# A hybrid encoder layer on one core: the mixer's blocks in another order, and an output operator kept in float32

## The chip, the cores and the metric

The kernel runs on one core of one Trainium2 chip, as one program launch. The metric is device time in microseconds (us): 1196.42 us is the median of 3 runs of the kernel before (1193.84 to 1198.22 us). Five engines each work through a queue of their own: TensorE (PE; its weight loads are listed apart as PEld), VectorE (DVE), ScalarE (ACT), GpSimd (POOL) and SyncE (SP). They wait for each other by semaphores, and an instruction that waits holds everything behind it on its engine. Transfers (DMAs) are issued from the queues of SP, ACT or POOL and run on 16 DMA engines.

## What is computed

One encoder layer over 512 tokens of width 1024: a SwiGLU feed-forward half step, a mixer with two parallel branches, a second feed-forward half step, and a per-layer embedding. The change lies in the mixer:

```
u = RMSNorm(h);  [q|k|v|x_ssm|g_attn|g_ssm] = u @ W_in        # 512,128,128,512,1024,1024 columns
y_attn = BlockGQA(AxialRoPE(RMSNorm(q)), AxialRoPE(RMSNorm(k)), v) @ W_attn_branch   # 8 q heads, 2 kv heads, of 64
z      = gelu(S5_fwd(x_ssm) + S5_bwd(x_ssm) + D*x_ssm)        # 32 groups of 16 channels, 64 complex states
y_ssm  = (z * sigmoid(z @ W_glu + b_glu)) @ W_ssm_branch
h      = h + (sigmoid(g_attn)*y_attn + sigmoid(g_ssm)*y_ssm) @ W_out
```

Everything is float32. The large products run in three passes (the helper `mm3`, L567): each operand is split into a rounded high part and the rest, and high x high, high x low and low x high are added up in PSUM.

## The kernel before

The layer runs in stages: FFN1 (the first 400 us or so of the trace; the parameters of the SSM are prepared beside it, and its operators written to DRAM), the in-projection with the mixer (to about 740 us), FFN2, and the embedding. All activations are kept transposed, features on the 128 partitions and 512 tokens along the free dimension.

**Tiles.** A weight chunk (`wchunk`, L556) is a 128 x 1024 float32 tile: SP issues its load, ACT casts the high part (L554), DVE subtracts for the low part (L555). There are 4 raw buffers and 4 high/low ones. A *gate* (L829) is one 128-column tile of g_attn or g_ssm: 24 matmuls of 128 x 512 (`pi`, L569 to L571), a DVE multiply into `ta` or `ts` (L833) and an ACT tanh (L834). There are 16 gates: 8 `ta`, 8 `ts`.

**The SSM.** The 32 groups are worked in 16 blocks of two (`ssm_prefetch` L436, `ssm_block` L453). A block loads its operators through SP: `wv` (L441), tables `tbl` (L444, L445), `wol` (L447) and `ml` (L449). PE makes `pv` from the input `U` and `wv` (24 products of 64 columns, six bf16 products for one float32 product, `mm6`). DVE rotates it (L471 to L473), runs two prefix scans (L481, L482) and rotates back (L485 to L487) into `E`. `split3` (L31) cuts E into three bf16 parts: ACT cast, DVE subtract `Er` (L34), ACT cast, DVE subtract (L36). PE then adds `U` x `ml` and `E` x `wol` in `py` (12 and 24 products), and ACT applies gelu into `Z`.

**The order of the mixer.** x_ssm, k and v and then q are projected; q and k are normalised and rotated. In program order there follow 8 gates, the transposes of q and k, the 16 blocks with one gate behind each of blocks 0, 2, 4 and 6, and the scores of head 0 behind block 14. `Z` is stored to DRAM (`zs_d`, 8 SP DMAs, L983), to come back with channels on the partitions (`zT`, L1032). Then come 8 heads; beside the values of head i and the scores of head i+1 runs `fill(i)`: four gates, the two halves of the GLU product and two of the four chunks of the SSM branch. Behind the heads stand the other two chunks of the SSM branch, the four of the attention branch (each merged in `attn_done`), W_out, FFN2 and the embedding.

**A head.** `scores` (L942): for each of 4 query tiles two matmuls `sc`, a row maximum `nb` on DVE (L957), a small DVE multiply by the query's norm `rq` (L958), and an exponential on ACT with bias `nb` and scale `rq` (L960). `values` (L988): 4 x 4 transposes `ppt`, their split `ph` (ACT) and `pl` (DVE), and 8 matmuls `po`. After every second head the reciprocals of the row sums go to DRAM (`r_d`, L966) and come back spread over 64 partitions (`R`, L1016), to scale the heads' output, which is then split into `oT`.

**What sets the order.** Each engine's queue is laid out by the scheduler of the language's Tile layer: it goes through the program with a timeline of its own and takes what is ready by it, earlier program order first; `tc.high_priority()` puts the blocks ahead. So code order and queue order differ, and the rows under the change show the queues. A tile with `bufs=1` can be loaded again only when the last reader of the old content is done.

Of the kernel before, what the change touches and what calls it, by code (L numbers as in the profile page):

```python
# [45 lines left out]
def ssm_params(tc, nc, pk_, px, dp, k):  # L46
# [6 lines left out]
    d["wo"] = dp.tile([NB, P, 3 * GB * 2 * P], BF16, name="d_wo")  # L53
# [264 lines left out]
    bds = [pw.tile([P, 2, GB, 2, CH], F32, name=f"bd{i}") for i in range(2)]  # L318
# [18 lines left out]
    for b in range(NB):  # L337
# [3 lines left out]
        wt = pw.tile([P, GB, 2, L, CH], F32, tag="wt", name=f"wo{b}")  # L341
# [20 lines left out]
        bd3 = pw.tile([P, 3, 2, GB, 2 * CH], BF16, tag="bd3", bufs=2, name=f"bd3{b}")  # L362
# [50 lines left out]
    for b in range(NB):  # L413
# [5 lines left out]
        wt = pw.tile([P, GB, 2, P], F32, tag="wt", name=f"wv{b}")  # L419
# [16 lines left out]
def ssm_prefetch(nc, sp, k, j):  # L436
# [81 lines left out]
def kernel(  # L518
# [331 lines left out]
    with tc.tile_pool(name="qp", bufs=1, reuse_waits="tile") as qp:  # L850
# [93 lines left out]
    def scores(hd):  # L944
# [25 lines left out]
    Z = sp.tile([P, G, NC_], F32, tag="U", name="Z")  # L970
    for j in range(NM):
        with tc.high_priority():
            py = ssm_block(nc, sp, ps, pre, U3, j)
        if j < NM - 1:
            pre = ssm_prefetch(nc, sp, kd, j + 1)
        S.activation(Z[:, j * GM:(j + 1) * GM].rearrange("p g c -> p (g c)"), py[:, :GM * NC_], AF.Gelu_apprx_tanh)
        if j % 2 == 0 and j // 2 < NG2:
            run(gate(NG1 + j // 2))
# [239 lines left out]
```

## Time and profile before

| | before |
|---|---|
| median of 3 runs | 1196.42 us (1193.84 to 1198.22) |
| the profiled execution | 1192.81 us |
| its span, first to last instruction | 1191.0 us |
| mean granted TensorE clock | 0.985 of full |
| PE busy | 1144.2 us (96%) |
| DVE busy | 772.2 us (65%) |
| ACT busy | 505.7 us (42%) |

The profile is one execution; its span is 1.8 us shorter than its own time, which is 3.6 us below the median. An engine is busy while it runs an instruction; waits, register and DMA-issuing instructions don't count. A row of waits names the engine and line that waited, and what came last. Line numbers are those of the kernel before, and "L43", "L36" and "L555" are lines in helpers, which is why the tile names matter more.

### The profile page before, as it was taken

How to read it: one execution, taken by the hardware profiler on the slowest of the kernel's cores; microseconds unless marked ns; L12 is line 12 of the kernel's file. 1: busy time of each engine (PE TensorE's matmuls, PEld its weight loads, DVE VectorE, ACT ScalarE, POOL GpSimd, SP SyncE). 2: the span in 40 equal slices, each digit the busy share in tenths (PEclk: the TensorE clock that was granted, in tenths of full speed). 3: DMA queues.
4: the chain of work that ended last, by engine and by line, in shares of the span. 5: the costliest groups of instructions: out<-in, count | busy, mean ns of one | idle time of the engine just before them, and what ended most of it. 6: DMA issues, size and time to landing. Idle time of an engine off the chain costs nothing.

```text
span 1191.0 us, 16469 instructions
## 1 busy us (share of the span) xinstructions
PE 1144.2 (96%) x6150; PEld 944.3 (79%) x6150; DVE 772.2 (65%) x1574; ACT 505.7 (42%) x917; POOL 44.1 (4%) x71
## 2 busy tenths in 40 slices
PE   8999979999999998998896999999999999999998
PEld 7888768888788887877675788888888888888886
DVE  4987789877589848998665857554443344444542
ACT  6484455445345436443565634333222223223331
POOL 1314200000000000000000000000000000000100
PEclk9999989999999999998997999999999999999999
DMA  8739856545968996886532125333223433223422
GB/s 193 165 100 302 255 192 204 160 141 113 268 228 264 302 177 190 232 267 201 144 69 57 45 78 174 93 94 101 85 66 97 141 89 106 79 72 98 154 59 53
DMA packets 258496, 175.97 MB, mean 148 GB/s; under 512 B 38928, under 2 KB 239824, under 8 KB 258416
## 3 DMA queue, kind: packets, MB, share of 16 engines
q1 hardware_dynamic: 252880, 157.41, 46.9%
q0 software_dynamic: 3920, 11.15, 3.5%
q10 hardware_dynamic: 1616, 6.36, 1.5%
q8 instruction: 48, 0.79, 0.3%
q14 instruction: 32, 0.26, 0.1%
HBM read 148.89 MB, written 37.58 MB: 157 GB/s over the span
## 4 chain that ended last, share of the span: by engine, by line
PE 76%; DMA 9%; DVE 5%; ACT 4%; SPq 3%; issue 2%; ACTq 0%; DVEq 0%
PE pg L569 7%; PE pg L570 7%; PE pg L571 7%; PE pd L569 7%; PE pd L571 7%; PE pd L570 7%; PE pu L571 5%; PE pu L569 5%; PE pu L570 5%; DMA ml<-d_m 3%; PE pi L569 2%; DMA d_tb<-tst 2%; PE pi L570 2%; PE pi L571 2%; SPq L411 1%
## 5 line engine op out<-in xcount | busy, mean ns | idle before, releaser
L723 DVE TENSOR_TENSOR t<-pu,rb 128x512 f32<-128x512 f32 x44 | 30.3, 689 | 84.6 <-PE pu L571 84.4
L721 DVE TENSOR_TENSOR t<-pg,rb 128x512 f32<-128x512 f32 x44 | 30.2, 687 | 51.6 <-PE pg L571 49.3
L554 ACT CAST ah<-t 128x512 fp32r<-128x512 f32 x44 | 27.4, 622 | 39.4 <-DVE t L724 38.5
L741 DVE SCALAR_TENSOR_TENSOR h<-pd,h 128x512 f32<-128x512 f32 x32 | 22.0, 687 | 30.4 <-PE pd L571 30.4
L722 ACT ACTIVATE t<-t 128x512 f32<-128x512 f32 x44 | 27.9, 633 | 24.3 <-DVE t L721 23.5
L555 DVE TENSOR_TENSOR pl<-ppt,ph 128x512 fp32r<-128x512 f32 x32 | 21.9, 684 | 17.6 <-ACT ph L554 17.6
L555 DVE TENSOR_TENSOR al<-t,ah 128x512 fp32r<-128x512 f32 x44 | 30.1, 685 | 4.2 <-ACT ah L554 4.0
L724 DVE TENSOR_TENSOR t<-t,t 128x512 f32<-128x512 f32 x44 | 30.3, 688 | 2.4
L960 ACT ACTIVATE p<-sc,nb,rq 128x512 f32<-128x512 f32 x32 | 24.8, 781 | 6.9 <-DVE nb L958 6.8
L554 ACT CAST ph<-ppt 128x512 fp32r<-128x512 f32 x32 | 18.6, 588 | 15.8 <-PE ppt L1000 15.4
L1123 POOL DMA_DIRECT2D pin<-in_p_dram x8 | 4.2, 530 | 556.1 <-PE pd L570 551.0
L1005 PE MATMUL po<-ph,vhl 128*128 128x512 f32 x32 | 14.0, 439 | 10.9 <-ACT ph L554 10.8
L579 ACT ACTIVATE xh<-h,gains 128x512 fp32r<-128x512 f32 x24 | 17.4, 723 | 16.7 <-DVE h L741 16.3
L957 DVE TENSOR_REDUCE nb<-sc 128x1 f32<-128x512 f32 x32 | 21.4, 682 | 1.0 <-PE sc L956 0.7
L43 PE MATMUL py<-U,ml 128*128 128x64 bf16 x192 | 10.8, 197 | 10.2 <-DMA ml<-d_m 10.2
L1000 PE MATMUL ppt<-ident,p 128*128 128x128 f32 x128 | 20.2, 272 | 0.2 <-ACT p L960 0.2
L1000 PEld LDWEIGHTS ppt<-ident,p 128*128 128x128 f32 x128 | 16.2, 140 | 4.4 <-ACT p L960 0.3
L580 DVE SCALAR_TENSOR_TENSOR xl<-h,gains,xh 128x512 fp32r<-128x512 f32 x24 | 17.9, 746 | 0.4
L43 PE MATMUL py<-E,wol 128*128 128x64 bf16 x384 | 17.6, 196 | 0.4 <-DVE E L36 0.4
L43 PEld LDWEIGHTS <-wv 128*128 128x128 bf16 x384 | 12.9, 100 | 6.1 <-issue 5.4
L43 PE MATMUL pv<-U,wv 128*128 128x64 bf16 x384 | 14.6, 196 | 3.2 <-DVE U L36 3.2
L43 PEld LDWEIGHTS <-ml 128*128 128x128 bf16 x192 | 7.8, 100 | 11.3 <-DMA ml<-d_m 11.1
(1970 smaller groups left out, 3892.2 us busy)
## 6 DMA issues: line engine op xcount, KB each, us to landing
w<-in_ffn_w_gate_dram SPq DMA_DIRECT2D x44, 512.0 KB
w<-in_ffn_w_up_dram SPq DMA_DIRECT2D x44, 512.0 KB
w<-in_w_in_dram SPq DMA_DIRECT2D x26, 512.0 KB
w<-in_ffn_w_down_dram SPq DMA_DIRECT2D x32, 384.0 KB
w<-in_ffn_w_down_dram SPq DMA_DIRECT2D x32, 320.0 KB
d_wo<-wo SPq DMA_DIRECT2D x8, 768.0 KB
d_wv<-wv SPq DMA_DIRECT2D x8, 768.0 KB
wv<-d_wv SPq DMA_DIRECT2D x16, 384.0 KB
```

The lines of the kernel that those rows point to most:

```text
L43: nc.tensor.matmul(o, a[i], b[j], start=start and n == 0, stop=stop and n == 5)
L554: S.copy(hi, src)
L555: V.tensor_sub(lo, src, hi.bitcast(F32))
L569: T.matmul(o, ah, bh, start=start, stop=False)
L570: T.matmul(o, ah, bl, start=False, stop=False)
L571: T.matmul(o, al, bh, start=False, stop=stop)
L721: V.tensor_mul(t1, gu[0], rb)
L722: S.activation(t1, t1, AF.Silu)
L723: V.tensor_mul(t2, gu[1], rb)
L724: V.tensor_mul(t1, t1, t2)
L960: S.activation(p_, sc, AF.Exp, bias=nb[:, t:t + 1], scale=rq[:, t, hd:hd + 1], accum_out=sm[:, t:t + 1])
L1000: T.transpose(pt[:, t * P:(t + 1) * P], pr[t][:, kt * P:(kt + 1) * P], ident)
```

## The change

Five things are changed.

1. **Output operator.** `d_wo` is kept in float32 (256 KB a block to load where it was 384 KB) and E is not split: a block has 4 float32 products with `wol` where it had 24 bf16 ones. `wv` has two buffers (before one). In the preparation `wt` has two buffers, and `bd` and `bd3` one instead of two.
2. **Query norm.** q is multiplied by `rq` (4 DVE multiplies of 128 x 512) before the transposes. The multiply of each row maximum by `rq` and the scale of the exponential are gone.
3. **Order.** 4 gates, then 12 SSM blocks with a gate behind every third of them (gates 4 to 7); block 0 is held back until the last q matmul is issued; then the q and k transposes, the last 4 blocks and the scores of head 0. Beside head i runs gate 8 + i. Behind the heads: `z_load`, the attention branch, the GLU, the SSM branch, which now merges (`ssm_done`).
4. **Store of Z.** In four groups of blocks, each of 8 DMAs of 16 x 8 x 64, 32 in all.
5. **Queues.** `zs_d`, `r_d`, `R`, `zT` and the reload of `h` are issued by POOL, no longer by SP.

```diff
-    d["wo"] = dp.tile([NB, P, 3 * GB * 2 * P], BF16, name="d_wo")
+    d["wo"] = dp.tile([NB, P, GB * 2 * P], F32, name="d_wo")
...
-    wv = sp.tile([P, 3, GM, 2 * P], BF16, tag="wv", name=f"wv{j}")
+    wv = sp.tile([P, 3, GM, 2 * P], BF16, tag="wv", bufs=2, name=f"wv{j}")
...
-    E3 = [sp.tile([P, 2, N], BF16, tag=f"E{i}", bufs=2, name=f"E3{j}_{i}") for i in range(3)]
-    split3(nc, sp, E, E3, "vv", f"Er{j}", 3)
...
-            mm6(nc, o, [wo[:, i, g, ri * P:(ri + 1) * P] for i in range(3)],
-                [e[:, ri, g * NC_:(g + 1) * NC_] for e in E3], False, ri == 1)
+            nc.tensor.matmul(o, wo[:, g, ri * P:(ri + 1) * P], E[:, ri, g * NC_:(g + 1) * NC_],
+                             start=False, stop=ri == 1)
...
-        for m in range(NG1):
+        for t in range(TT):
+            V.tensor_mul(qs[t], qs[t], rq[:, t].unsqueeze(2).broadcast_to([P, NH, HD]))
+        for m in range(KT // 2):
             run(gate(m))
+        def ssm(j):
+            nonlocal pre
+            with tc.high_priority(), (tc.issue_after(last_q.ins) if j == 0 else ExitStack()):
+                py = ssm_block(nc, sp, ps, pre, U3, j)
...
+            if j % 4 == 3:
+                gs = slice((j - 3) * GM, (j + 1) * GM)
+                for l in range(L):
+                    nc.gpsimd.dma_start(zv[l][:, gs], Z[l * CH:(l + 1) * CH, gs])
+        for j in range(NM - JL):
+            ssm(j)
+            if j % 3 == 0:
+                run(gate(KT // 2 + j // 3))
...
-            V.tensor_mul(nb[:, t:t + 1], nb[:, t:t + 1], rq[:, t, hd:hd + 1])
-            S.activation(p_, sc, AF.Exp, bias=nb[:, t:t + 1], scale=rq[:, t, hd:hd + 1], accum_out=sm[:, t:t + 1])
+            S.activation(p_, sc, AF.Exp, bias=nb[:, t:t + 1], accum_out=sm[:, t:t + 1])
...
-            nc.sync.dma_start(r_d[hd // 2].rearrange("h (t p) -> p h t", p=P), s2)
+            nc.gpsimd.dma_start(r_d[hd // 2].rearrange("h (t p) -> p h t", p=P), s2)
...
-                nc.sync.dma_start(R[i * HD:(i + 1) * HD], r_d[hd // 2][i].partition_broadcast(HD))
+                nc.gpsimd.dma_start(R[i * HD:(i + 1) * HD], r_d[hd // 2][i].partition_broadcast(HD))
...
-            nc.sync.dma_start(zT, zs_d[m * P:(m + 1) * P])
+            nc.gpsimd.dma_start(zT, zs_d[m * P:(m + 1) * P])
...
     for hd in range(NH):
-        run(values(hd), fill(hd), *([scores(hd + 1)] if hd < NH - 1 else []))
-    for i in range(NH, 2 * KT - NG1 - NG2 + 6):
-        run(fill(i))
+        run(values(hd), gate(KT + hd), *([scores(hd + 1)] if hd < NH - 1 else []))
+    z_load()
     for mc in range(4):
         run(half(w["w_attn_branch"][0], mc, ohl, attn_done))
+    for mc in range(2):
+        run(half(w["ssm_glu_w"][0], mc, [z[1:] for z in zs[1:]], glu_done))
+    for mc in range(4):
+        run(half(w["w_ssm_branch"][0], mc, yhl, ssm_done))
```

**PE where the first block begins.** Before, block 0's first products stand in the middle of the 96 matmuls `pq` of the q projection (the last 48 of them follow):

```order
L571 MATMUL pq_4518<-w_330h,xl_373 128x512
L569 MATMUL pq_4518<-w_330h,xh_374 128x512
L570 MATMUL pq_4518<-w_330l,xh_374 128x512
L571 MATMUL pq_4518<-w_330h,xl_375 128x512
L43 LDWEIGHTS wv_4150
L43 MATMUL pv_5068<-U_4161,wv_4150 128x64
L43 LDWEIGHTS wv_4150
L43 MATMUL pv_5068<-U_4160,wv_4150 128x64
...
L43 LDWEIGHTS ml_5160
L43 MATMUL py_5244<-U_4159,ml_5160 128x64
L569 MATMUL pq_4515<-w_331h,xh_376 128x512
L570 MATMUL pq_4515<-w_331l,xh_376 128x512
```

Now they stand behind the last `pq`, block 0 and block 1 (the second `wv`) in turn:

```order
L569 MATMUL pq_4518<-w_332h,xl_381 128x512
L567 MATMUL pq_4518<-w_332h,xh_382 128x512
L568 MATMUL pq_4518<-w_332l,xh_382 128x512
L569 MATMUL pq_4518<-w_332h,xl_383 128x512
L43 LDWEIGHTS wv_4150
L43 MATMUL pv_4863<-U_4161,wv_4150 128x64
L43 LDWEIGHTS wv_4920
L43 MATMUL pv_4963<-U_4161,wv_4920 128x64
```

The products that read `U` moved from the middle of the q projection to its end, and the first two blocks are interleaved. (The next rows of both are more of the same 24 products, then those with `ml`.)

**The queue that carries r_d, R and zT.** Before, on SP, from the load of the first two zT tiles on (weights `w` stand in between):

```order
L1032 DMA zT_7220<-zs_d 128x512
L1032 DMA zT_7226<-zs_d 128x512
L966 DMA r_d_5064<-s_428_6890 128x8x1
L1032 DMA zT_7232<-zs_d 128x512
L1032 DMA zT_7238<-zs_d 128x512
L1016 DMA R_7209<-r_d_5064 64x512 x2
L564 DMA w_7824<-in_w_attn_branch_dram 128x4x256
L564 DMA w_7874<-in_w_attn_branch_dram 128x4x256
L966 DMA r_d_5065<-s_483_7122 128x8x1
L1016 DMA R_7494<-r_d_5065 64x512 x2
```

Now, on POOL, from the second `r_d` on:

```order
L989 DMA r_d_5898<-s_420_6331 128x8x1
L1029 DMA R_6638<-r_d_5898 64x512 x2
L989 DMA r_d_5899<-s_475_6555 128x8x1
L1029 DMA R_6862<-r_d_5899 64x512 x2
L989 DMA r_d_5900<-s_530_6779 128x8x1
L1042 DMA zT_7068<-zs_d 128x512
L1042 DMA zT_7074<-zs_d 128x512
L1042 DMA zT_7080<-zs_d 128x512
L1042 DMA zT_7086<-zs_d 128x512
L1029 DMA R_7060<-r_d_5900 64x512 x2
```

Before, two of the four zT stand behind the second `r_d`; now all four stand directly behind the fourth, and ahead of the last `R`. No weights stand in this queue.

**ACT where the z tiles are cast.** Before, beside heads 2 and 3 (`p` is the exponential, `ph` the cast of transposed probabilities, `ob` the copy of a head's upper half):

```order
L960 ACTIVATE p_7088,s_428_6890<-sc_7083,nb_7008,rq 128x512
L554 CAST oT_6981<-of_6860 128x512
L554 CAST z_7222<-zT_7220 128x512
L554 CAST w_617h<-w_7626 128x1024
L554 CAST z_7228<-zT_7226 128x512
L834 ACTIVATE ts_5059<-ts_5059 128x512
L554 CAST z_7234<-zT_7232 128x512
L554 CAST ph_7047<-ppt_7042 128x512
L554 CAST z_7240<-zT_7238 128x512
L554 CAST ph_7071<-ppt_7066 128x512
L960 ACTIVATE p_7128,s_483_7122<-sc_7123,nb_7121,rq 128x512
L960 ACTIVATE p_7152,s_483_7122<-sc_7147,nb_7121,rq 128x512
```

Now, beside the last two heads:

```order
L552 CAST ph_6876<-ppt_6871 128x512
L552 CAST w_618h<-w_7194 128x1024
L552 CAST z_7070<-zT_7068 128x512
L1024 COPY ob_6859<-po_6755 64x512
L552 CAST ph_6907<-ppt_6902 128x512
L833 ACTIVATE ts_5893<-ts_5893 128x512
L552 CAST z_7076<-zT_7074 128x512
L552 CAST z_7082<-zT_7080 128x512
L552 CAST z_7088<-zT_7086 128x512
L552 CAST oT_6866<-of_6749 128x512
L552 CAST ph_6930<-ppt_6925 128x512
L552 CAST ph_6953<-ppt_6948 128x512
```

The four casts `z` moved from there to the last two heads, and casts `ph` that the last products `po` read stand behind them: one behind the first z, the others behind all four.

## Rows read from the trace of the kernel before

**Rows 1.** The page: busy us, share and instructions; PE clock in 40 slices.
```profile
PE 1144.2 (96%) x6150; PEld 944.3 (79%) x6150; DVE 772.2 (65%) x1574; ACT 505.7 (42%) x917; POOL 44.1 (4%) x71
PEclk9999989999999999998997999999999999999999
```
**Rows 2.** Windows: us, busy of each engine (instructions), clock, DMA share, GB/s.
```profile
456.00:581.00 125.00, 114.34 (x1286) 96.01 (x1284) 112.94 (x268) 56.11 (x154) 0.76 (x1) 0.96 0.75 222
490.00:510.00 20.00, 18.14 (x230) 14.82 (x228) 19.53 (x62) 7.83 (x15) 0.00 (x0) 1.00 0.96 281
...
530.00:550.00 20.00, 15.04 (x170) 13.30 (x167) 17.64 (x39) 8.11 (x18) 0.00 (x0) 0.83 0.66 201
...
624.00:641.00 17.00, 5.53 (x14) 3.73 (x13) 5.57 (x13) 3.75 (x8) 0.00 (x0) 0.60 0.37 69
641.00:705.00 64.00, 63.13 (x311) 50.99 (x311) 46.76 (x80) 37.73 (x71) 0.00 (x0) 1.00 0.23 58
820.00:960.00 140.00, 140.00 (x619) 115.99 (x618) 57.34 (x70) 37.38 (x46) 0.00 (x0) 1.00 0.33 97
```
**Rows 3.** What PE waited for, 408 to 700 us: total, times, longest.
```profile
PE po L1005 <- ACT ph L554: 10.8, 2, 10.5
PE py L43 <- DMA ml<-d_m: 10.2, 7, 3.5
PE pv L43 <- DVE U L36: 3.2, 1, 3.2
```
**Rows 4.** What the SP queue waited for, whole span.
```profile
SPq L1016 <- DMA r_d<-s: 38.0, 4, 10.3
...
SPq L444 <- DVE te L485: 32.5, 12, 5.3
```
**Rows 5.** DVE by line, 456 to 581 us: busy, mean ns | idle before.
```profile
L36 DVE TENSOR_TENSOR E<-Er,E 128x256 bf16<-128x256 f32 x16 | 6.7, 421 | 1.2 <-ACT E L35 1.0
L34 DVE TENSOR_TENSOR Er<-vv,E 128x256 f32<-128x256 f32 x16 | 6.7, 419 | 3.1 <-ACT E L33 3.1
L833 DVE TENSOR_TENSOR ta<-pi,rb 128x512 f32<-128x512 f32 x8 | 5.5, 682 | 0.0
...
L957 DVE TENSOR_REDUCE nb<-sc 128x1 f32<-128x512 f32 x3 | 2.0, 681 | 0.0
...
L555 DVE TENSOR_TENSOR w_351l<-w,w_351h 128x1024 fp32r<-128x1024 f32 x1 | 1.2, 1226 | 0.5 <-ACT w_351h L554 0.5
```
**Rows 6.** The page's groups: products and transposes on PE.
```profile
L43 PE MATMUL py<-E,wol 128*128 128x64 bf16 x384 | 17.6, 196 | 0.4 <-DVE E L36 0.4
...
L1000 PE MATMUL ppt<-ident,p 128*128 128x128 f32 x128 | 20.2, 272 | 0.2 <-ACT p L960 0.2
```
**Rows 7.** Timeline of PE, the last block's: start, us, instruction, count.
```profile
580.55 0.51 PE L43 MATMUL py<-E,wol 128*128 128x64 bf16 x12
```
**Rows 8.** Timeline of the SP queue, 615 to 700 us.
```profile
618.59 1.02 SPq L1032 DMA_DIRECT2D zT<-zs_d  x2
619.72 0.37 SPq L966 DMA_DIRECT2D r_d<-s  x1
620.13 1.40 SPq L1032 DMA_DIRECT2D zT<-zs_d  x2
...
691.62 1.09 SPq L1016 DMA_DIRECT2D R<-r_d  x2
```
**Rows 9.** Timeline of ACT, 615 to 640 us.
```profile
621.33 0.62 ACT L554 CAST z<-zT 128x512 fp32r<-128x512 f32 x1 [1.43 <-DMA zT<-zs_d]
...
633.83 0.62 ACT L554 CAST z<-zT 128x512 fp32r<-128x512 f32 x1 [9.87 <-DMA zT<-zs_d]
```
**Rows 10.** Transfers that POOL issued in FFN1 (tile d_a): ns min/median/max; landing.
```profile
L251 POOL DMA_DIRECT2D d_a<-d_at x16: 630/632/672, 87.7 to 120.2; - x16
...
DMA to landing us min/median/max: 6.1/9.7/15.7
```
**Rows 11.** DVE by line beside attention, 581 to 703 us.
```profile
L958 DVE TENSOR_TENSOR nb<-nb,rq 128x1 f32<-128x1 f32 x31 | 4.2, 150 | 0.1
```

More of the change, by code (lines that the diff above doesn't have):

```diff
@@ L317, in ssm_params @@
     kt = sm([P, 2, G, CH], "kt", pool=pk_)
-    bds = [pw.tile([P, 2, GB, 2, CH], F32, name=f"bd{i}") for i in range(2)]
+    bds = [pw.tile([P, 2, GB, 2, CH], F32, name=f"bd{i}") for i in range(1)]
     for bd in bds:
@@ L340, in ssm_params @@
         y4 = lambda t: t[:, gs].unsqueeze(2).broadcast_to(sh)
-        wt = pw.tile([P, GB, 2, L, CH], F32, tag="wt", name=f"wo{b}")
+        wt = pw.tile([P, GB, 2, L, CH], F32, tag="wt", bufs=2, name=f"wo{b}")
         m1 = pw.tile(sh, F32, tag="m1", name=f"m1o{b}")
@@ L361, in ssm_params @@
             nc.scalar.copy(bd[ps, :, :, dr], bb[ps, :, gs])
-        bd3 = pw.tile([P, 3, 2, GB, 2 * CH], BF16, tag="bd3", bufs=2, name=f"bd3{b}")
+        bd3 = pw.tile([P, 3, 2, GB, 2 * CH], BF16, tag="bd3", bufs=1, name=f"bd3{b}")
         split3(nc, pw, bd.rearrange("p r g d c -> p r g (d c)"), [bd3[:, i] for i in range(3)], "r3", f"bdr{b}", 2)
@@ L418, in ssm_params @@
         nc.sync.dma_start(br, b_d[:, :, gs])
-        wt = pw.tile([P, GB, 2, P], F32, tag="wt", name=f"wv{b}")
+        wt = pw.tile([P, GB, 2, P], F32, tag="wt", bufs=2, name=f"wv{b}")
         m1 = pw.tile([P, GB, P], F32, tag="m1", name=f"m1v{b}")
@@ L510 @@
 SSMW = 512
-NG1, NG2 = 8, 4
+JL = 4
 SIDE = (5.5, 4.5, 3)
@@ L570, in mm3 @@
         T.matmul(o, ah, bl, start=False, stop=False)
-        T.matmul(o, al, bh, start=False, stop=stop)
+        return T.matmul(o, al, bh, start=False, stop=stop)
     def xg_tiles(tagp, n):
@@ L825, in proj_tok @@
                     tk = slice(t * P, (t + 1) * P)
-                    mm3(banks[t][:, :n], xg[kk][0][:, tk], xg[kk][1][:, tk], wh[:, k], wl[:, k],
-                        kk == 0, kk == KT - 1)
+                    last = mm3(banks[t][:, :n], xg[kk][0][:, tk], xg[kk][1][:, tk], wh[:, k], wl[:, k],
+                               kk == 0, kk == KT - 1)
+        return last
     def gate(m):
@@ L836, in gate @@
         return proj_T(GA0 + m * P, done)
+    hb = mp.tile([P, 4], F32, name="hb")
+    nc.gpsimd.dma_start(hb, w["ssm_glu_b"][0].rearrange("(m p) -> p m", p=P))
+    V.tensor_scalar_mul(hb, hb, 0.5)
     ts = []
@@ L965, in scores @@
             V.reciprocal(s2, s2)
-            nc.sync.dma_start(r_d[hd // 2].rearrange("h (t p) -> p h t", p=P), s2)
+            nc.gpsimd.dma_start(r_d[hd // 2].rearrange("h (t p) -> p h t", p=P), s2)
     prs, sums2 = {}, {}
     r_d = [dp.tile([2, SEQ], F32, name=f"r_d{j}") for j in range(NH // 2)]
[L970 to L978, printed above, removed]
+    for j in range(NM - JL, NM):
+        ssm(j)
         if j == NM - 2:
             run(scores(0))
-    zv = zs_d.rearrange("(g c) (l n) -> l c g n", c=CH, l=L)
-    for l in range(L):
-        nc.sync.dma_start(zv[l], Z[l * CH:(l + 1) * CH])
     sx.close()
@@ L1025, in z_load @@
         xs_ = lambda k, c, name, dt=F32: slot(xp, f"x{k}{c}", 1, name, dt)
-        hb = at.tile([P, 4], F32, name="hb")
-        nc.gpsimd.dma_start(hb, w["ssm_glu_b"][0].rearrange("(m p) -> p m", p=P))
-        V.tensor_scalar_mul(hb, hb, 0.5)
         zs.append((hb, xs_))
@@ L1057, in glu_done, with attn_done @@
         split(yhl[m][0], yhl[m][1], tz)
+    def attn_done(m, pg):
+        V.scalar_tensor_tensor(ta[m], ta[m], 1.0, pg, add, mul)
+    mg = []
     def ssm_done(m, pg):
         V.scalar_tensor_tensor(ts[m], ts[m], 1.0, pg, add, mul)
-    def fill(i):
-        ng = 2 * KT - NG1 - NG2
-        if i < ng:
-            return gate(NG1 + NG2 + i)
-        if i < ng + 2:
-            if i == ng:
-                z_load()
-            return half(w["ssm_glu_w"][0], i - ng, [z[1:] for z in zs[1:]], glu_done)
-        if i < ng + 6:
-            return half(w["w_ssm_branch"][0], i - ng - 2, yhl, ssm_done)
-        return iter(())
-    mg = []
-    def attn_done(m, pg):
-        V.scalar_tensor_tensor(ta[m], ta[m], 1.0, pg, add, mul)
         mt = slot(at, "of", 3, "mt")
```

20 lines of the change are left out of this document (13 added, 7 removed).

## The prediction, made before the changed kernel ran

> **What bounds the kernel now.** I read the page first: PE is busy for 96% of the span and its granted clock is 9 tenths or more in nearly every slice [rows 1]. So time is to be had only where PE waits or its clock falls. The windows show how a stretch in which PE is the bound looks: at 820 to 960 us it is busy without a gap at full clock, 619 instructions in 140 us, 0.226 us for one 128x512 matmul [rows 2]. Against that two stretches stand out. From 456 to 581 us, the SSM blocks, DVE is busy for 112.9 of 125 us, PE for 114.3 at a clock of 0.96 [rows 2]: the blocks are held by DVE and by their loads (in the 20 us from 490 the DMA engines are 96% busy at 281 GB/s), and gates fill PE up. From 624 to 641 us PE works 5.5 of 17 us at a clock of 0.60 [rows 2]. The waits of PE name what ended these gaps: 10.8 us for the cast `ph`, 10.2 us in 7 waits for `ml`, 3.2 us for the split of U [rows 3].
>
> The long one is a transfer seen through ACT's queue. The `ph` that PE wants stands on ACT behind a cast of zT that waits 9.87 us [rows 9]. Two zT issued at 618.6 us were there at 621.3; the next two, issued at 620.1 just behind an `r_d`, only at 633.8, 13.7 us later [rows 8, 9]. The SP queue shows what `r_d`, 1024 single words, does: each of four loads of R waits about 10 us for it [rows 4]. What stands behind an `r_d` on its queue, or needs it, is about 10 us late.
>
> **The SSM stage.** DVE's work there, from its rows: it loses the split of E, 6.7 + 6.7 = 13.4 us; three gates less by the stage's end (9 are done by then, now 12) take away three `ta` multiplies, 2.0, and three weight splits of 1.22, 3.7; it gains four multiplies of q by rq, 2.7 by the row of the same size (0.682), and some four row maxima more of that size, 2.7, because scores of head 1 move in [rows 5]. 112.9 - 13.4 - 2.0 - 3.7 + 2.7 + 2.7 = 99.2 us. That is the floor. Of the 12.1 us in which DVE idled, 1.2 + 3.1 us were waits for ACT inside the split [rows 5], which go; about 8 stay, so 107 us if the loads keep up. The loads: 125 us at 222 GB/s are 27.8 MB [rows 2]; 16 blocks load 128 KB less each, 2.1 MB, so 25.7 MB are left, 92 us at 281 GB/s and 116 us at the mean rate. Second buffers for `wv` let SP issue further ahead, which speaks for the faster rate. I take 106 us, so the stage ends at 562 us, where before its last product ran at 580.6 us [rows 7]; bounds 99 and 125 us (unchanged).
>
> The 19 us are not all gain, because PE does less in them: three gates of 24 matmuls are put off, 72 x 0.226 = 16.3 us, against about 2.6 us of scores and transposes of head 1 done earlier. Net 13.7 us move to stretches where PE has no gap (63.1 of 64 us at 641 [rows 2]). Gain 19 - 13.7 = 5.3 us. In it is the 3.2 us wait of the first `pv` in the middle of the q projection [rows 3]: U is late there, and now the whole projection stands ahead of it. DVE still has to make U, but PE has 48 more matmuls, 10.9 us, to run meanwhile.
>
> The float32 products: the nearest rows are 17.6 us for 384 bf16 products of 64 columns and 20.2 us for 128 float32 transposes of 128 columns, 0.158 us each [rows 6]. 64 products cost 64 x 0.158 = 10.1 us if each is one such instruction and 20.2 us if it is two. So -7.5 to +2.6 us. I take the dear end and still count nothing, because PE is not the bound of this stage: its gates are put off, and if it became the bound, 2.6 us would be due.
>
> **The z detour, gone and back.** Now no cast of zT stands ahead of work in the middle of attention. The 17 us window held 14 instructions, 3.2 us at 0.226: 14 us come back. But the four zT stand on POOL directly behind the fourth `r_d`, and on ACT one cast z stands ahead of a `ph` and all four ahead of three more that the last head needs. The fourth `r_d` is issued when the last exponential is done; by the rows above what follows it lands some 13 us later. PE has meanwhile the rest of the last gate, the products of head 6, and three of four k of the first attention chunk, some 30 instructions or 7 us. So a wait of about 5 us: 0 if the zT don't feel the `r_d` on this queue, 8 with the clock falling as it did at 624 us.
>
> POOL's queue is one that the mixer of before doesn't use for this. Its nearest row is FFN1's transfer `d_a`: 0.63 us to issue, 6.1 to 15.7 us to land [rows 10]. The 32 stores of Z cost 32 x 0.63 = 20 us of POOL, spread over the stage, and nothing needs them until the end; the 8 that SP issued no longer stand ahead of weights. The same goes for SP's four waits for `r_d` [rows 4], but the weights behind them were early: PE has no gap beside them, so I count nothing.
>
> The Trainium skill bears on this queue ("SBUF — State Buffer", section "SBUF: two separate sides"): descriptors of a DMA that GpSimd issues are written by software, which VectorE can lock out while it runs certain operations, an fp32 copy within SBUF above all; queues of SP and ACT are immune. The trace of before rather speaks against it: the issues of `d_a` took 630 to 672 ns each, with no long one [rows 10]. By the rule the sum would be that of the third rival below, 1197 us, by the row 1185 us.
>
> **The last head.** Before, the last `R` was asked for at 691.6 us [rows 8] while SSM-branch and attention-branch products of other heads were still there. Now the attention branch comes at once; its k = 3 needs the last `oT`, and only four PSUM banks let PE run ahead. The copy `ob` and the cast (0.62 us as ACT's cast of this size [rows 9]), the add, the multiply by R and the subtract (0.68 each [rows 5]) make 3.3 us in a row, 4 with some clock. Before, about 25 products of the branch covered it. Bounds 0 (the GLU, ordered behind, is brought forward) and 12 us (R waits for its `r_d`).
>
> **Within the heads.** 31 multiplies of 150 ns [rows 11] leave DVE's way from maximum to exponential: 4.2 us off a DVE that is busy for 46.8 of 64 us [rows 2], worth about 1 us to PE. Beside each head runs a gate of 24 matmuls as before four gates and four half branches of 24 did: no change. FFN1, where preparation gets one buffer more here and one less there, and FFN2 I leave at nothing, +-2 us.
>
> **Sum.** -5.3 - 14 + 5 + 4 - 1 = -11.3 us. Against the profiled execution's own 1192.8 us that is 1181.5; the median of before lies 3.6 us above it, so I predict 1185 us.
>
> **Rivals.**
> *The stage keeps its pace (slower).* The blocks form a chain: a table buffer is free only after DVE's `te`, for which SP waited 32.5 us in 12 waits [rows 4], and the loads behind it then make PE wait for `ml` [rows 3]. If this loop and not DVE's sum sets 7.8 us a block, the stage takes 125 us again, with three gates fewer done: +13.7 - 14 + 5 + 4 - 1 = +8, 1204 us. It decides once the stage takes 120 us or more. For it: from 530 to 550 us DVE was busy for 17.6 of 20 us and PE for 15.0, so neither was the bound there. Against: 19.5 of 20 us of DVE at 490 [rows 2].
> *Everything clears (faster).* DVE's floor is reached (99 us, 7 more), and zT does not feel the `r_d`: -11.3 - 7 - 5 = -23, 1173 us. For it: wv is loaded two blocks ahead. Against: 281 GB/s must hold throughout.
> *POOL's queue is slow (no change).* If zT and the last R land as late as the largest `d_a`, 15.7 us, instead of its median, 9.7 us [rows 10], each costs 6 us more, all of it uncovered: -11.3 + 12 = +0.7, 1197 us. Against: DVE's rows here are two-operand float32 operations, no copies [rows 5].
> *The change does not do what it says.* The queues show that it mostly does; but the transposes of q and k stand behind a later block, and a scheduler may have spent the room. Then no change, 1195 us.
>
> **Chances.** Forecast 0.50, pace kept 0.17, all clears 0.15, POOL slow 0.13, no effect 0.05. 0.5% is 6 us, about what can be told from no change: 1190.4 and 1202.4 us are the bounds. Faster: 0.45 of the forecast's half and 0.15 = 0.60. Same: 0.05 + 0.02 + 0.11 + 0.05 = 0.23. Slower: 0.15 + 0.02 = 0.17. The range from 1168 to 1204 us leaves out about a tenth on each side; the forecast's own is 1178 to 1191.
>
> **What would show it.** Right: the blocks' last E product near 562 us; DVE above 90% busy until then; no gap of PE with the clock at 0.6 in the middle of attention; one of some 5 us near its end, ended by `ph` behind a cast of zT, and one of 3 to 4 us at k = 3 of the attention branch. Wrong: a stage of 120 us or more with waits for `ml` and `tbl`; R or zT landing over 14 us after their issue; or gaps in FFN1, which I left alone.

## The result, and the profile after

The changed kernel takes 1203.86 us (median of 7 runs, 1200.74 to 1209.64); its ratio to the kernel before is 1.0085, 95% interval 1.0063 to 1.0108. It is slower by about 10 us, where 1185 us and faster were forecast. The profiled execution is the longest of the seven (1209.64 us, span 1207.9), so its distance to the profile before, 16.9 us, is more than the medians show; below, sizes come from medians and places from the trace.

The page after, against [rows 1]:

```profile
PE 1158.9 (96%) x5894; PEld 954.6 (79%) x5894; DVE 764.0 (63%) x1513; ACT 492.4 (41%) x887; POOL 75.2 (6%) x127
PEclk9999989999999999998999799999999999999999
```

The windows after, the same stretches as in [rows 2]:

```profile
456.00:581.00 125.00, 111.29 (x1026) 94.01 (x1025) 109.69 (x249) 55.21 (x142) 16.72 (x32) 0.94 0.71 206
624.00:641.00 17.00, 14.87 (x70) 11.14 (x70) 10.65 (x17) 9.66 (x24) 1.62 (x3) 1.00 0.17 40
641.00:705.00 64.00, 53.64 (x225) 41.60 (x225) 31.89 (x46) 23.79 (x42) 4.49 (x8) 0.89 0.28 72
```

The hole at 624 us is gone, as forecast. In its place the stretch at 641 us, without a gap before, is 10 us short of PE work, at a clock of 0.89. The waits of PE from 408 to 715 us, against [rows 3]:

```profile
PE po L1018 <- ACT ph L552: 7.0, 3, 6.4
PE py L493 <- DMA wol<-d_wo: 5.1, 4, 2.9
PE pg L567 <- ACT oT L552: 2.8, 1, 2.8
PE pk L567 <- DVE X L884: 2.6, 2, 2.0
```

The first is zT again. POOL's timeline, then ACT's, near the last heads, against [rows 8, 9]:

```profile
654.49 0.93 POOL L989 DMA_DIRECT2D r_d<-s  x1 [13.14 <-DVE s L988]
655.41 1.79 POOL L1042 DMA_DIRECT2D zT<-zs_d  x3
```

```profile
669.19 0.62 ACT L552 CAST z<-zT 128x512 fp32r<-128x512 f32 x1 [10.15 <-DMA zT<-zs_d]
```

13.8 us from the issue of zT to its first cast: the number of before, 13.7 us. PE's timeline shows what it costs there, and the wait for the last oT behind it:

```profile
671.08 0.80 PE L1018 MATMUL po<-ph,vhl 128*128 128x512 f32 x1 [6.41 <-ACT ph L552]
671.67 0.63 PE L567 MATMUL pg<-oT,w_612h 128*128 128x512 f32 x1
...
687.25 1.22 PE L567 MATMUL pg<-oT,w_609h 128*128 128x512 f32 x2 [2.77 <-ACT oT L552]
```

A matmul listed with 0.63 us stands 0.43 us behind the one before it (at full clock 0.23): after each of the two holes the clock is at its lower level (granted 0.50 of full, 1.2 GHz, from 671.2 to 675.9 us and from 687.3 to 692.9 us), for 10 and 13 matmuls, which makes 2 and 2.6 us more.

The fourth wait stands in a place that the forecast passed over. The rows of the tile X, the x part of the in-projection, after:

```profile
L884 DVE TENSOR_TENSOR X<-pi,rb x4: 681/688/692, 433.3 to 440.6; 128x512 f32<-128x512 f32 x4
L885 SPq DMA_DIRECT2D xs_d<-X x4: 319/352/1650, 434.0 to 441.3; - x4
...
  DMA xs_d<-X: 5.3, 1
```

Before, X ran from 425.2 to 428.7 us. So the mixer starts 8 us late here, ahead of anything that the change reorders. 3.6 of the 8 us stand already at the end of FFN1 (its last product `pd` starts at 405.3 us, before at 401.7), and such a difference isn't the change: over all runs below that start lies between 402.3 and 407.9 us, whatever the buffers. What comes behind it differs by more: from the last `pd` to the first matmul of q are 41.2 us here and 35.9 us before. And the SSM stage, by the first and last starts of its first and last products:

```profile
L43 PE MATMUL pv<-U,wv x384: 189/193/204, 468.3 to 554.4; 128*128 128x64 bf16 x192
L493 PE MATMUL py<-vv,wol x128: 217/276/455, 477.7 to 575.0; 128*128 128x64 f32 x128
```

It takes 106.7 us, the length that was forecast (106), but from 468 us instead of 456, and ends at 575 instead of 562 us. It is one profile: in those of e1, e2, e3 and e5 below, with the same blocks, it takes 101.6 to 102.9 us. DVE works for 95.7 of the 106.7 us, 90%.

### The profile page after: what moved, and what is told of

Read it like the earlier page. It is cut to its first block, busy times and chain, and to the rows that moved or that the text cites. A ratio compares the mean times of both kernels' runs of the same rounds, so it can differ in the third digit from the quotient of the medians.

```text
span 1207.9 us, 15906 instructions
## 1 busy us (share of the span) xinstructions
PE 1158.9 (96%) x5894; PEld 954.6 (79%) x5894; DVE 764.0 (63%) x1513; ACT 492.4 (41%) x887; POOL 75.2 (6%) x127
## 4 chain that ended last, share of the span: by engine, by line
PE 74%; DMA 11%; DVE 6%; ACT 4%; SPq 3%; issue 2%; POOL 0%; ACTq 0%; DVEq 0%
PE pg L567 7%; PE pg L568 7%; PE pg L569 7%; PE pd L567 6%; PE pd L569 6%; PE pd L568 6%; PE pu L569 5%; PE pu L567 5%; PE pu L568 5%; DMA w<-in_ffn_w_down_dram 2%; PE pi L567 2%; DMA wol<-d_wo 2%; PE pi L568 2%; PE pi L569 2%; SPq L411 1%
## 5 line engine op out<-in xcount | busy, mean ns | idle before, releaser
L553 DVE TENSOR_TENSOR pl<-ppt,ph 128x512 fp32r<-128x512 f32 x32 | 21.9, 686 | 20.2 <-ACT ph L552 20.2
L553 DVE TENSOR_TENSOR al<-t,ah 128x512 fp32r<-128x512 f32 x44 | 30.3, 688 | 4.3 <-ACT ah L552 4.0
L981 DVE TENSOR_REDUCE nb<-sc 128x1 f32<-128x512 f32 x32 | 21.7, 685 | 11.2 <-PE sc L980 11.1
L493 PE MATMUL py<-vv,wol 128*128 128x64 f32 x128 | 21.7, 301 | 5.7 <-DMA wol<-d_wo 5.1
L935 POOL DMA_DIRECT2D zs_d<-Z x32 | 16.7, 530 | 148.6 <-ACT Z L930 148.6
L493 PEld LDWEIGHTS py<-vv,wol 128*128 128x128 f32 x128 | 19.0, 213 | 6.7 <-issue 3.8
L983 ACT ACTIVATE p<-sc,nb 128x512 f32<-128x512 f32 x32 | 21.9, 690 | 3.9 <-DVE nb L981 2.0
L1019 PE MATMUL po<-pl,vhl 128*128 128x512 f32 x32 | 14.0, 437 | 2.7 <-DVE pl L553 2.6
```

Source lines behind the costliest of these rows:

```text
L493: nc.tensor.matmul(o, wo[:, g, ri * P:(ri + 1) * P], E[:, ri, g * NC_:(g + 1) * NC_], start=False, stop=ri == 1)
L553: V.tensor_sub(lo, src, hi.bitcast(F32))
```

## The experiments

All ratios are to the kernel before, measured beside each run (its median 1193.7 to 1195.9 us); 0.1% is 1.2 us. A difference between two runs is taken from their ratios. "Mends" are edits of the changed kernel.

| run | median us | ratio (95% interval) | first pv to last E product, us |
|---|---|---|---|
| before | 1195.9 | 1 | 451.9 to 580.9 = 129.0 |
| changed | 1203.9 | 1.0085 (1.0063 to 1.0108) | 468.3 to 575.0 = 106.7 |
| e1_prep | 1197.3 | 1.0025 (1.0006 to 1.0043) | 460.5 to 562.6 = 102.1 |
| e2_zt_sp | 1204.9 | 1.0088 (1.0064 to 1.0112) | 467.1 to 569.5 = 102.4 |
| e3_zt_glu | 1205.3 | 1.0096 (1.0073 to 1.0119) | 464.3 to 565.9 = 101.6 |
| e4_bf16 | 1224.7 | 1.0254 (1.0231 to 1.0278) | 465.5 to 592.8 = 127.3 |
| e5_rt | 1199.1 | 1.0047 (1.0029 to 1.0066) | 466.6 to 569.5 = 102.9 |
| e6_rt_prep_tail | 1190.2 | 0.9966 (0.9945 to 0.9986) | 464.2 to 568.2 = 104.0 |
| e7_before_rt | 1194.3 | 0.9998 (0.9977 to 1.0019) | 453.3 to 584.4 = 131.1 |
| e8_before_f32 | 1187.8 | 0.9952 (0.9935 to 0.9968) | 451.6 to 569.8 = 118.2 |
| e9_before_f32_rt | 1187.6 | 0.9945 (0.9926 to 0.9964) | 454.4 to 572.5 = 118.1 |
| e10_no_hold | 1196.7 | 1.0036 (1.0018 to 1.0054) | 451.2 to 555.1 = 103.9 |
| e11_ml_once | 1196.1 | 1.0016 (0.9999 to 1.0033) | 465.4 to 568.3 = 102.9 |
| e12_gates | 1191.2 | 0.9970 (0.9952 to 0.9987) | 461.1 to 566.9 = 105.8 |
| e13_before_f32_rt_tail | 1186.9 | 0.9934 (0.9910 to 0.9958) | 452.7 to 573.0 = 120.3 |
| e14_old_order | 1190.8 | 0.9960 (0.9941 to 0.9979) | 461.1 to 565.0 = 103.9 |

**The preparation's buffers (e1_prep).** The changed kernel with `wt`, `bd` and `bd3` buffered as before:

```diff
-    bds = [pw.tile([P, 2, GB, 2, CH], F32, name=f"bd{i}") for i in range(1)]
+    bds = [pw.tile([P, 2, GB, 2, CH], F32, name=f"bd{i}") for i in range(2)]
...
-        wt = pw.tile([P, GB, 2, L, CH], F32, tag="wt", bufs=2, name=f"wo{b}")
+        wt = pw.tile([P, GB, 2, L, CH], F32, tag="wt", name=f"wo{b}")
...
-        bd3 = pw.tile([P, 3, 2, GB, 2 * CH], BF16, tag="bd3", bufs=1, name=f"bd3{b}")
+        bd3 = pw.tile([P, 3, 2, GB, 2 * CH], BF16, tag="bd3", bufs=2, name=f"bd3{b}")
```

> The changed kernel with the preparation's buffers as before (wt one buffer, bd two, bd3 two); everything else as changed. Theory A (the single bd and bd3 buffers make the preparation late; the last d_wv is written at 420 instead of 406 us, which pushes norm, X and U back): the last d_wv is written near 406 to 410 us, the first pq matmul starts near 440 instead of 446.5 us, and the time falls by 4 to 8 us against the changed kernel (1203.9), to 1196 to 1200. Rival B (the lateness ahead of the mixer is the variation of one profiled run, or comes from the other loads): pq still starts near 446 us, time within 2 us of the changed kernel.

Theory A. The ratio falls from 1.0085 to 1.0025, 7.2 us (+-3.5, from the two intervals). The writes of `d_wv`, the preparation's last product, in the changed kernel and then here:

```profile
L426 SPq DMA_DIRECT2D d_wv<-wv x8: 338/339/562, 316.8 to 420.3; - x8
```

```profile
L426 SPq DMA_DIRECT2D d_wv<-wv x8: 338/342/2302, 308.6 to 408.1; - x8
```

(Before: 307.1 to 406.1 us.) From 400 to 450 us, before, changed and here:

```profile
400.00:450.00 50.00, 48.35 (x260) 41.20 (x259) 28.08 (x72) 19.66 (x49) 1.28 (x3) 1.00 0.98 222
```

```profile
400.00:450.00 50.00, 45.16 (x244) 38.01 (x243) 37.27 (x86) 22.66 (x51) 2.39 (x4) 1.00 0.94 263
```

```profile
400.00:450.00 50.00, 49.94 (x268) 42.76 (x267) 30.34 (x76) 20.28 (x49) 2.39 (x4) 1.00 0.96 230
```

In the changed kernel DVE works for 37.3 us there, against 28.1 before and 30.3 here, and PE misses 4.8 us of work that it doesn't miss here. From the last `pd` of FFN1 to the first matmul of q are 40.2 to 41.9 us in the five runs with the changed buffers (changed, e2, e3, e4, e5) and 35.7 to 36.2 us in all the others. That is 4 to 6 us, within the interval of the 7.2. Which of the three tiles matters was not tried apart.

**Where zT waits (e2, e3, e5, e7).** First the queue alone:

```diff
-            nc.gpsimd.dma_start(zT, zs_d[m * P:(m + 1) * P])
+            nc.sync.dma_start(zT, zs_d[m * P:(m + 1) * P])
```

> The changed kernel with the four zT loads on SP's queue; r_d and R stay on POOL. FFN1 and the in-projection are those of the changed kernel. Theory A (zT is late because it stands behind the fourth r_d on its queue): zT lands 3 to 5 us after its issue instead of 13.8, the 6.4 us wait of PE for ph and the slow clock behind it (2.2 us) go, the time falls by 6 to 9 us to 1195 to 1198. Rival B (the loads of zT themselves are slow, or ACT's order holds ph): the wait stays above 4 us, time within 3 us of 1203.9.

Neither time nor wait moved much, which is rival B by its numbers: beside the last heads PE waits 6.9 us for `ph` in three pieces, the longest 4.5. SP's timeline and ACT's:

```profile
649.48 3.27 SPq L1042 DMA_DIRECT2D zT<-zs_d  x4
```

```profile
657.39 0.62 ACT L552 CAST z<-zT 128x512 fp32r<-128x512 f32 x1 [8.97 <-DMA zT<-zs_d]
...
663.15 0.62 ACT L552 CAST z<-zT 128x512 fp32r<-128x512 f32 x1 [4.66 <-DMA zT<-zs_d]
```

On a queue without `r_d` zT is still late: the first cast comes 7.9 us and the second 13.7 us behind the first issue. POOL issued `r_d` at 648.95 us, and it landed 13.1 us later, at 662.1. Its window behind it (the last two columns: share of the DMA engines' time, GB/s):

```profile
653.00:662.00 9.00, 7.04 (x33) 5.15 (x31) 1.89 (x3) 1.10 (x2) 0.00 (x0) 1.00 0.70 25
```

The engines are 70% busy and move 25 GB/s. So my theory, the place on the queue, fell. Nor did other work ahead help, with the GLU's chunks in front of the attention branch's and zT on SP:

```diff
+    for mc in range(2):
+        run(half(w["ssm_glu_w"][0], mc, [z[1:] for z in zs[1:]], glu_done))
     for mc in range(4):
         run(half(w["w_attn_branch"][0], mc, ohl, attn_done))
-    for mc in range(2):
-        run(half(w["ssm_glu_w"][0], mc, [z[1:] for z in zs[1:]], glu_done))
```

> As the run with zT on SP's queue, and the GLU product stands ahead of the attention branch instead of behind it. Theory A (nothing covers the last R and oT because the attention branch comes at once and four PSUM banks let PE run no further): the wait for oT (2.8 us) with the slow clock behind it (2.6 us) goes, and the time falls by 4 to 6 us more than in that run, to 1190 to 1193. Rival B (the last head's own chain of transposes, casts and products sets the end): the wait moves to another instruction, and the time is within 2 us of that run.

The time is that of e2, as rival B had it. PE now waits 8.2 us for `z` itself, and the wait for `oT` stays at 2.8 us: the scheduler pulled the GLU ahead of the last head instead of into the hole. Then `r_d` itself, turned on PE so that it is written in 8 rows:

```diff
-            V.reciprocal(s2, s2)
-            nc.gpsimd.dma_start(r_d[hd // 2].rearrange("h (t p) -> p h t", p=P), s2)
+            st_ = bank("pt", uid("st"))
+            T.transpose(st_[:2 * TT, :P], s2.rearrange("p h t -> p (h t)"), ident)
+            rs = a0.tile([2 * TT, P], F32, tag="rs", bufs=1, name=uid("rs"))
+            V.reciprocal(rs, st_[:2 * TT, :P])
+            nc.gpsimd.dma_start(r_d[hd // 2].rearrange("h (t p) -> (h t) p", p=P), rs)
```

> The changed kernel, but the reciprocals of a pair of heads are turned on PE first (one transpose, 128x8 to 8x128) and written to r_d as 8 rows of 512 bytes instead of 1024 single words; all queues as changed. Theory A (the single-word write of r_d holds the DMA engines themselves for about 10 us, so whatever is in flight beside it is late, on SP's queue as on POOL's): zT lands within 5 us, PE's wait for ph near the last heads falls from 6.4 to under 2 us with no slow clock behind it, time 1194 to 1198. Rival B (the loads of zT are slow by themselves): the wait stays above 4 us and the time within 3 us of the changed kernel's 1203.9.

Theory A in the trace: zT is cast without a wait, `R` follows `r_d` by 2 us instead of 10 or more, and the wait for `ph` is 0.5 us. POOL's timeline:

```profile
665.53 0.52 POOL L992 DMA_DIRECT2D r_d<-rs  x1 [8.74 <-DVE rs L991]
667.67 1.06 POOL L1032 DMA_DIRECT2D R<-r_d  x2 [1.62 <-DMA r_d<-rs]
```

The time falls by 4.5 us (+-3.6, from the intervals), less than the 6 to 10 us expected. But the edit did two things: the scheduler also put zT ahead of the fourth `r_d` (zT is issued from 652.4 to 656.3 us, that `r_d` at 665.5), and in e7, e6, e9, e13 and e14 no `r_d` is in flight beside zT either. So these runs show what is won when the two don't overlap. That zT would be quick beside an `r_d` of 8 rows is not shown. The same edit in the kernel before, on SP's queue:

> The kernel before, with the turned reciprocals written to r_d as 8 rows of 512 bytes, on SP's queue as there. Theory A (the single-word write is the cause of the 17 us stretch at 624 us in which PE waits for zT): the 10.5 us wait goes, time 1193.8 - 10 to 14 = 1180 to 1184. Rival B (zT waits for its buffers or for stores of Z): the stretch stays, time within 3 us of 1193.8.

Neither, and this is the more instructive result. The wait of 10.5 us is gone, and the time is the same. The stretch around it, and the one behind the last head, before and then with the edit:

```profile
621.00:641.00 20.00, 8.53 (x31) 6.22 (x30) 8.28 (x16) 6.38 (x12) 0.00 (x0) 0.66 0.43 73
...
701.00:721.00 20.00, 20.00 (x89) 16.16 (x88) 14.83 (x22) 7.01 (x10) 0.00 (x0) 1.00 0.46 139
```

```profile
621.00:641.00 20.00, 14.88 (x61) 11.16 (x60) 12.69 (x23) 10.32 (x22) 0.00 (x0) 0.83 0.33 101
...
701.00:721.00 20.00, 17.24 (x70) 13.57 (x69) 13.23 (x19) 7.22 (x10) 0.00 (x0) 0.91 0.30 87
```

6.3 us come back at once, not 14: shorter waits for `ph`, `pl` and `ts` of 1.6 to 1.8 us remain in this part of the kernel. 2.8 us are lost again at the end: the SSM branch's products are done by 694 us there and no longer cover the last oT.

**The operator (e4, e8).** Back to bf16 parts in the changed kernel (the edits of the change to `d_wo`, `wol` and E undone, `wv` with one buffer), and the float32 operator alone in the kernel before:

```diff
+    E3 = [sp.tile([P, 2, N], BF16, tag=f"E{i}", bufs=2, name=f"E3{j}_{i}") for i in range(3)]
+    split3(nc, sp, E, E3, "vv", f"Er{j}", 3)
...
-            nc.tensor.matmul(o, wo[:, g, ri * P:(ri + 1) * P], E[:, ri, g * NC_:(g + 1) * NC_],
-                             start=False, stop=ri == 1)
+            mm6(nc, o, [wo[:, i, g, ri * P:(ri + 1) * P] for i in range(3)],
+                [e[:, ri, g * NC_:(g + 1) * NC_] for e in E3], False, ri == 1)
```

> The changed kernel with the output operator in bf16 parts as before (E split, 24 bf16 products a block, 384 KB wol, wv one buffer); order and queues as changed. Theory A (the float32 operator shortens the SSM stage because DVE loses the split and the loads 128 KB a block): the stage from the first pv to the last E product takes 118 us or more instead of 107 us, the time rises by 5 to 12 us to 1209 to 1216. Rival B (the float32 products cost PE as much as DVE gains, 21.7 us of PE against 17.6 and 5 us of waits for wol): the stage takes 104 to 112 us and the time is within 3 us of 1203.9 or below it.

> The kernel before with the float32 output operator alone (d_wo in float32, no split of E, 4 float32 products a block; buffers, order and queues as before). Theory A (the operator is a gain by itself: DVE loses 13.4 us, ACT as much, the loads 2.1 MB in a stage that they hold): the last E product ends 8 to 14 us earlier than 581 us, time 1182 to 1188. Rival B (it is a gain only in the changed order, where block follows block; among 12 gates PE is the bound and pays 21.7 us instead of 17.6): time within 3 us of 1193.8 or above.

Theory A both times, but in the changed kernel with more than its size: the time rises by 20 us, where 5 to 12 were expected. The bf16 blocks in a row take 127.3 us, about as long as before, with three gates less beside them; from 480 to 580 us PE works for 79.3 us at a clock of 0.83, in the changed kernel for 87.0 at 0.93. The 20 us are those of the operator and of the second `wv` buffer together, which e4 takes back with it; e8 has one `wv` buffer. In the kernel before the operator gives 5.7 us (3.8 to 7.8), the edge of the 6 to 12 expected: the last E product comes 11 us earlier (569.8), but PE pays for part of it. Its busy time from 400 to 740 us rises from 310.6 to 319.4 us, so it loses 8.8 us less there, and the dearer products take 2.6 of them. The products there, against [rows 6]:

```profile
L493 PE MATMUL py<-vv,wol 128*128 128x64 f32 x128 | 20.2, 279 | 0.8 <-DVE vv L486 0.6 <-DMA wol<-d_wo 0.2
```

64 products show as 128 records and take 20.2 us, as the dear end of the bound had it, against 17.6.

**All three mends (e6), and with a later edit of the stage (e10 to e12, e14).** In e6 the first chunk of the GLU is queued behind the last product of attention:

```diff
+    run(half(w["w_attn_branch"][0], 0, ohl, attn_done))
+    with tc.issue_after(last_po[0].ins):
+        run(half(w["ssm_glu_w"][0], 0, zx, glu_done))
```

> The changed kernel with three mends: the preparation's buffers as before, the turned reciprocals, and the first half of the GLU product queued on PE behind the last product of attention, the attention branch's other chunks behind it. If the three costs are separate they add up: 6.6 us (preparation), 6 to 8 us (zT), 4 to 5 us (wait for the last oT and the slow clock behind it), so 1185 to 1188, faster than the kernel before (1193.8). If the time hides in a common bound (loads or the last head's chain), it stays above 1190.

1190.2 us, 14 us (+-4) below the changed kernel. That is short of the 1185 to 1188 of the sum and just above the rival's 1190, but faster than the kernel before. PE's wait for oT falls from 2.8 to 0.3 us. In e10 block 0 is free to go ahead, `with tc.high_priority():` alone:

> The run with the three mends, but block 0 is not held behind the last q matmul. Theory A (the stage could not start before 464 us, which is what the forecast left out: it took the place where block 0 stood before): the first pv stands in the middle of the q projection again, at about 452 us, PE waits there 2 to 4 us for U, and the last E product comes 4 to 8 us earlier than 568.5; time 1184 to 1187. Rival B (the stage is held by its loads, which start no earlier): the last E product within 2 us of 568.5, time within 2 us of 1190.2 or above.

Neither: the last E product comes 13 us earlier, at 555.1 us (10 us, counted from the first q matmul), and the kernel is 8 us slower. This shows that the end of the stage is not what is to be counted. While the blocks ran, PE did less else (181 gate matmuls between the first q matmul and the last E product, counted in the trace, against 216 in e6 and 288 before), and the early start hurt the q projection, here and then in e6:

```profile
450.00:480.00 30.00, 25.78 (x260) 21.97 (x259) 27.81 (x62) 14.40 (x48) 0.00 (x0) 0.84 0.78 228
```

```profile
450.00:480.00 30.00, 30.00 (x237) 25.19 (x235) 25.39 (x48) 21.68 (x85) 0.00 (x0) 1.00 0.70 196
```

PE misses 4.2 us of work there and runs at a clock of 0.84, which over 30 us is another 4 to 5 us: about the size of the whole loss.

e11 keeps one `ml` for all blocks:

```diff
-    nc.sync.dma_start(mm, d["m"][:, :, j * GM:(j + 1) * GM])
+    if "ml0" not in k:
+        k["ml0"] = sp.tile([P, 3, GM, P], BF16, tag="m", bufs=1, name=f"ml{j}")
+        nc.sync.dma_start(k["ml0"], d["m"][:, :, j * GM:(j + 1) * GM])
+    mm = k["ml0"]
```

> The run with the three mends, but every block uses block 0's ml: 15 loads of 192 KB are left out (2.9 MB of some 25 MB in the stage), so the blocks' direct term is wrong; the instructions of PE, DVE and ACT are the same in number. Theory A (loads set the stage's pace): the stage from the first pv to the last E product falls from 104 us by 8 to 12 us. Rival B (DVE sets it): it falls by less than 3 us.

Rival B by its number: with 2.9 MB less to load the stage takes 102.9 instead of 104.0 us, though 24 gate matmuls fewer (192) stand beside it. The volume of the loads does not set its pace. That DVE does is not shown by it: DVE works for 91.6 of the 102.9 us. (The time rose by 6 us; the scheduler laid the gates otherwise.) e12 moves three gates into the stage:

```diff
+        if j < NM - 1:
+            run(gate(KT + j - (NM - JL)))
```

> The run with the three mends, but gates 8, 9 and 10 run beside the last SSM blocks, gates 11 to 15 beside heads 0 to 4, and the GLU product beside heads 5 and 6; the first chunk of the SSM branch covers the last oT. Theory A (the reordering lost because three gates, 16.3 us of PE, left a stage in which PE waits for one in which it does not): the stage grows by less than 6 us, and the time falls by 6 to 12 us to 1178 to 1184. Rival B (the last blocks have no PE time to spare): the stage grows by the 16 us and the time stays within 3 us of 1190.2.

Inconclusive: of 72 matmuls only 19 landed ahead of the last E product (235 against 216) and 14 score matmuls left it; the time is that of e6. e14 is e6 in the order of before, all else kept (the heads' fill and the merge as before too):

```diff
-        for m in range(KT // 2):
+        for m in range(KT):
             run(gate(m))
...
-    for j in range(NM - JL, NM):
+    for j in range(NM):
         ssm(j)
+        if j % 2 == 0 and j // 2 < 4:
+            run(gate(KT + j // 2))
```

> The changed kernel with the three mends, but in the order of before: 8 gates, q and k transposes, 16 blocks with gates 8 to 11 behind blocks 0, 2, 4 and 6, gates 12 to 15, the GLU and two SSM chunks beside the heads, the attention branch last. Kept from the change: float32 operator, second wv buffer, block 0 behind the last q matmul, query norm on q, Z in four groups, POOL's queue. Theory A (the order is what loses: with the blocks in a row PE finds less to do in the stage, 216 gate matmuls against 288): PE's lost time in the stage falls from 19 to 14 to 16 us, time 1181 to 1185. Rival B (the other parts lose it, the later start of block 0 or POOL's queue): time within 3 us of 1190.2.

Rival B: 1190.8 us, the time of e6. With the float32 operator the order as written is worth nothing either way, as far as 0.3% can tell; the scheduler put 235 gate matmuls into the stage, so the order of e8 (284) is not wholly back and the test is a weak one.

**On the kernel before (e9, e13).** The operator with the turned reciprocals, then with the last SSM chunk queued behind the last product of attention:

```diff
+    run(fill(NH))
+    with tc.issue_after(last_po[0].ins):
+        run(fill(NH + 1))
```

> The kernel before with the float32 output operator and the turned reciprocals. The operator alone gave 1187.8, the reciprocals alone nothing in time though the 10.5 us wait went: the last head then stood uncovered (2.9 us and a slow clock). If these add up as they stood: 1187 to 1188. If the SSM branch's products still cover the last oT here, the wait at 620 to 630 us (11 us in the run with the operator alone) comes out of the time: 1178 to 1182.

> The kernel before with the float32 output operator, the turned reciprocals, and the last chunk of the SSM branch queued on PE behind the last product of attention. Theory A (in the run without that last edit the gain of the reciprocals was lost at the last oT: 2.9 us of wait and 2.6 us of slow clock at 696 us): that wait goes, time 1187.6 - 4 to 5 = 1182 to 1184. Rival B (the gain was lost spread over the heads): time within 2 us of 1187.6.

1187.6 and 1186.9 us: the wait at the last oT (2.8 us) goes in e13, and no more than 1 us with it, so rival B. What the reciprocals free is lost again in small waits of the heads: PE waits 5.8 us for `pl` in e13, 3.1 in e9. e13 has the lowest time, 0.66% (0.42 to 0.90) below the kernel before; the operator alone (0.48%) makes most of that, and the intervals of e8, e9 and e13 overlap.

## Why the prediction was wrong

The sum said -11.3 us and about +10 were measured. Two of its terms make nearly all of these 21 us, the first two here.

- **"FFN1 I leave at nothing": the step that failed first.** One buffer less for `bd` and `bd3` was seen and not priced. The preparation ran 12 us later than with the old buffers (its last `d_wv` at 420.3 against 408.1 us), into the in-projection, and with DVE's work there X came late. Measured: +7.2 us where 0 was put (e1).
- **"The z detour, gone": the largest term, mis-sized.** Counting the whole 17 us window gave 14 us. Where the wait alone was removed (e7), 6.3 us came back in that window and nothing in the time (-0.2 us, +-2.5): waits of other heads and of the last oT stood behind it. A hole in a chain that runs through ACT, DVE and PE is not worth its length.
- **"and back": right place, cause misread.** The stall of zT came as forecast, between a `ph` and the fourth `r_d`: 6.4 us against 5, with the slow clock 8.4 against 8 at most. But the rival sum, 0 "if the zT don't feel the `r_d` on this queue", took the queue for the cause; e2 shows that another queue feels it too. Without the overlap 4.5 us come back (e5).
- **The last head:** 2.8 us of wait against 3.3, as reasoned, and 2.6 us of slow clock behind it, against 0.7 allowed.
- **The stage.** Its length was right within a few us (101.6 to 106.7 against 106), its start wrong: I put it at 456 us, where before block 0 already ran (from 451.9), though the order of PE showed it behind all of the q projection. In every run in which block 0 is held back the first `pv` comes 21.7 to 21.8 us behind the first q matmul; that would have been 459.4 us before. So of the 12.3 us by which it came late 3.4 are that, 5.3 the preparation and 3.6 the later end of FFN1 in this profile. More basic, the gain was counted at the stage's end, less the deferred gates; e10 ends its stage 13 us earlier and loses 8 us. What counts is what PE loses over the whole mixer, by waits and by a slow clock. In time the operator gives 5.7 us in the kernel before, the order as written next to nothing (e14). That 5.7 is near the 5.3 of the forecast is luck: it was measured among the gates of the old order, with none put off.
- **The rivals.** The slower one (pace kept) did not happen, the stage went from 129 to 107 us; POOL's slowness hardly (`R` waited up to 12.8 us for `r_d`, on SP up to 10.3 [rows 4]; the 32 stores of Z took 0.53 to 0.57 us each to issue, none long). The slowdown came by a path that no rival described, though the list of signs came near it with "gaps in FFN1, which I left alone".

The sum of what was measured: -5.7 (operator) + 7.2 (preparation) + 4.5 (zT beside `r_d`) = +6; the cover of the last head may give about 2.5 us more (e6 against e1 and e5 together), but that is within their noise. That would be 8 to 9 of the 10 us. Each of these terms is known to 2 to 4 us only, and the operator's was measured in the other kernel, so the agreement proves little. The rest stays open, and so does whether the held block, POOL's queue, the query norm or the earlier load of the GLU's bias costs anything: e14, which has them all, is some 3 us slower than e13, but the intervals overlap.

## What to carry to other kernels

Price every buffer that a change takes away, also in a stage that it is not about: a preparation that ends just in time has no slack to give. On an engine that is 96% busy, count its lost time from end to end and not when a stage ends; a stage that ends sooner with less other work beside it need not gain (e10). When one long wait is to go, ask what stands behind it on the next engine; its length, with the slow clock behind it, is the upper end of the gain.

## What the runs showed of the hardware

With a DMA in flight that writes 1024 single words, loads on another queue were late too (e2). The 16 DMA engines were then 70% busy at 25 GB/s, and a 256 KB load on SP took 7.9 us and more to its first use, against 2.7 us for the two issued ahead of the `r_d` in the kernel before [rows 8, 9] and 3 us from issue to landing in e5, where no `r_d` was in flight. As 8 rows of 512 bytes the same 4 KB landed 2.1 us after their issue in e5, where the single words took some 10 to 13 us. The Trainium skill says that transfers issued by different engines run on the same 16 DMA engines and interleave ("DMA: Bandwidth & Descriptors", section "Issuing engines are not separate DMA queues"); e2 agrees, with 25 GB/s beside it.
